# A scan that multiplies the sample state's decay on ScalarE, loads B, C and decay rows earlier, and squares later

## The chip, the cores and the metric

The kernel runs on one core of one Trainium2 chip. The metric is the device time of one launch in microseconds (us); the time before is the median of three runs. TensorE (PE in the profile, PEld its weight loads) multiplies matrices, VectorE (DVE), ScalarE (ACT) and GpSimd (POOL) do the elementwise work, SyncE (SP) issues the DMAs. Each has a queue of its own that runs in order. SBUF and PSUM are the two on-chip memories, PSUM the one that TensorE writes.

## The reference, cut to what matters

One layer of a decoder, for a prompt of 1024 tokens and a sample group of 8 sequences with one new token each, which share the weights. A projection of the normed input gives q, k, v for a dilated window attention and z, x, B, C, dt for a state-space scan (32 heads of 64, 8 groups of B and C, state size 128). The scan of the prompt runs in 8 chunks of 128 tokens; for the sample it is one step from a given state. Then come the gates, an output projection and an MLP, all in f32.

```python
# prompt, per chunk, group and head; a_cs is the running sum of dt * A
lmat = exp(segsum(a))                                   # decay from row s to row l
y_diag = einsum('bcgels,bcsgep->bclgep', cb * lmat, x * dt)
states = einsum('bclgn,bclgep->bcgepn', B, x * dt * exp(a_cs[last] - a_cs))
y_off  = einsum('bclgn,bcgepn->bclgep', C, state_before) * exp(a_cs)
# sample, one token: state (heads, 64, 128) of each of 8 sequences
state = state * exp(dt * A) + (x * dt) outer B          # written out as ssm_sample
y = state . C + d_skip * x
# both: y = rmsnorm_per_group(y * silu(z)) * norm_g
```

## The kernel before

All dense products run as `Dense` jobs: one job makes 128 output features for all tokens, in three chunks of 384, 384 and 264 tokens. A chunk is 24 matmuls into one PSUM tile (`mm`, three of them): each f32 operand is split into a high and a low part and three of the four products are added (lines 140 to 142). Weights are loaded (`wraw`), cast on ScalarE (`whi`, L94) and subtracted on GpSimd (`wlo`, L95), one job ahead. A chunk ends with its eviction (`evac`).

One chunk is one step of a clock. Everything that is not dense is written as generators (`sides`); after each chunk `pump` advances them, up to 4 turns a step in the scan, in the order of the list. `rest(n)` lets n steps pass. So the code sets where the small matmuls of the sides stand between the chunks. Only TensorE's order is taken as written (`manual_schedule`). The order on the other engines and on SyncE's DMA queue is made by the framework, which may run an instruction before others that stand ahead of it in the code, as far as data and buffers allow; a tile with `bufs=n` waits until its n-th predecessor is no longer needed.

The scan stage (474 to some 1275 us of the span) runs over 8 groups of 4 heads. In a group the dense work is 2 z jobs, then 4 x jobs of the next group (x, x, B, C; for five groups one gate job among them): 21 steps, some 108 us. The x eviction is a 4-tap causal convolution: ScalarE makes the first tap (L819), VectorE adds three (L823), ScalarE the tanh (L832), VectorE the product (L833). Results stand in `ck` tiles. Next to it run three generators for each group (`ssd_sides`):

- `chunks` goes through the 8 prompt chunks. `load(c)` fetches the decay row `ar` (4 heads x 128 tokens, the same row to all 128 partitions, 256 KB) from `ac_d` (L906, five buffers). `prep(c)` transposes x and B and multiplies C by B on TensorE, scales x on VectorE (L925, L928), and makes the decay matrix in place: four relus and an exp on ScalarE (L932, L934), a product on GpSimd (L935). `state(c)` makes the carried state (L941, L947), `out(c)` the outputs (L956, L960, then L964 to L967).
- `decode` updates the sample state, in four pairs of sequences `bh` and two halves t. B and C go through DRAM (`bc_d`) and come back to all partitions (`bc`, L867, two buffers); the state comes in `hst` (L872, four buffers) and goes out again (L892). VectorE makes dx = x dt (L884), ScalarE tmp = B dx (L887), VectorE hst = hst decay + tmp (L888) and the product with C (L890).
- `finish_` gates each of the three token chunks (`gate`: GpSimd's product L978, its store, ScalarE's squares L980, VectorE's sum L981) and two steps later adds the squares up on TensorE (`sums`).

Before the scan, the attention stage makes scores, softmax and values of 8 blocks for each of 6 head pairs (`attn_side`): L545 adds the bias, takes the maximum and writes it into the tile `o`, which also gets the values and is then stored to `att_d`; there are four such tiles. After the scan, the output projection's last jobs feed the second norm (`norm2`): the squares of 8 feature blocks are added in `ssq` (L1371), summed over features on TensorE (`rstd_cols`, L284), turned into a factor on VectorE, spread by transposes (L1420), and applied to 8 blocks (L1423 to L1429), which the MLP's first jobs read.

Of the kernel before, what the change touches and what calls it, by code (L numbers as in the profile page):

```python
# [7 lines left out]
F32 = mybir.dt.float32  # L8
# [3 lines left out]
OP = mybir.AluOpType  # L12
# [28 lines left out]
def _trunk(ctx, tc, nc, I, O):  # L41
# [109 lines left out]
    def rest(n):  # L151
        t = clock[0] + n
        while clock[0] < t:
            yield 'wait'
# [334 lines left out]
    def attn_side(u, tiles):  # L489
# [42 lines left out]
        def scores(j):  # L532
            nk = 128 * len(kbs[j])
            b0 = 128 if (g < 2 and nk == 128) else 0
            st = sts[j] = at.tile([128, 2, 256], F32, name="st", tag="st", bufs=4)
            o = os_[j] = at.tile([128, 132], F32, name="o", tag="o", bufs=4)
            lm = o[:, 128:132]
            nm = at.tile([128, 2], F32, name="nm", tag="nm", bufs=2)
            ps = [ps_(), ps_()]
            for hb in range(2):  # L540
                T.matmul(ps[hb][:, :nk], qt[hb * 64:(hb + 1) * 64, j * 128:(j + 1) * 128],  # L541
                         kt[hb * 64:(hb + 1) * 64, kbs[j][0] * 128:kbs[j][0] * 128 + nk],
                         start=True, stop=True)
            for hb in range(2):
                V.tensor_tensor_reduce(st[:, hb, :nk], ps[hb][:, :nk], bias[:, hb, b0:b0 + nk], 1.0, -3e38,  # L545
                                       OP.add, OP.max, lm[:, 2 + hb:3 + hb])
            V.tensor_scalar(nm, lm[:, 2:4], -1.0, None, op0=OP.mult)
            for hb in range(2):
                A.activation(st[:, hb, :nk], st[:, hb, :nk], AF.Exp, bias=nm[:, hb:hb + 1],
                             accum_out=lm[:, hb:hb + 1])  # L550
# [240 lines left out]
    def x_jobs(gi, tl):  # L791
# [45 lines left out]
            jobs.append(Dense(w_in, 0, col, 128, hx_, evac, halo=HALO))  # L837
        return jobs

    def ssd_sides(gi, tl):  # L840
        X, Z = tl['x'], tl['z']
        hs = slice(4 * gi, 4 * gi + 4)
# [6 lines left out]
        def decode():  # L849
            while tl['nx'] < 12:  # L850
                yield 'wait'
            yield from rest(1)
            tl['fin']()
            yield from rest(1)
            rb = sa.tile([11, 256], F32, name="rb", tag="tail", bufs=2)[:8].rearrange("p (k n) -> p k n", k=2)
            ps = ps_()
            T.transpose(ps[:8, 0:128], X[2][2][:, sam], ident)
            T.transpose(ps[:8, 128:256], X[3][2][:, sam], ident)
            V.tensor_copy(rb.rearrange("p k n -> p (k n)"), ps[:8, :256])
            dma(bc_d[gi].rearrange("k b n -> b k n"), rb)  # L860
            got = {}

            def load(bh):
                if bh > 3:
                    return
                bc = sd.tile([128, 2, 2, 128], F32, name="bc", tag="bc", bufs=2)
                dma(bc, dap(bc_d, gi * 2048 + bh * 256, [[0, 128], [1024, 2], [128, 2], [1, 128]]))  # L867
                hs_ = []
                for t in range(2):
                    r0 = bh * 2 * 262144 + (4 * gi + 2 * t) * 8192  # L870
                    hst = sd.tile([128, 2, 128], F32, name="hst", tag="hst", bufs=4)
                    dma(hst, dap(ws, r0, [[128, 128], [262144, 2], [1, 128]]))  # L872
                    hs_.append((r0, hst))
                got[bh] = bc, hs_
            load(0)
            yield from rest(2)
            for bh in range(4):
                load(bh + 1)
                bc, hs_ = got[bh]
                for t, (r0, hst) in enumerate(hs_):  # L880
                    ds = dsel[:, 2 * gi + t, :]
                    dx = sd.tile([128, 8], F32, name="dx", tag="dx", bufs=2)
                    xcol = X[t][2][:, 256 + 2 * bh:258 + 2 * bh]
                    V.tensor_tensor(dx[:, :2], xcol, ds[:, 2 * bh:2 * bh + 2], op=OP.mult)  # L884
                    for i in range(2):
                        tmp = sd.tile([128, 128], F32, name="tmp", tag="tmp", bufs=3)
                        A.mul(tmp, bc[:, 0, i, :], dx[:, i:i + 1])  # L887
                        V.scalar_tensor_tensor(hst[:, i, :], hst[:, i, :], ds[:, 8 + 2 * bh + i:9 + 2 * bh + i],  # L888
                                               tmp, op0=OP.mult, op1=OP.add)
                        V.tensor_tensor_reduce(tmp, hst[:, i, :], bc[:, 1, i, :], 1.0, 0.0,  # L890
                                               OP.mult, OP.add, dx[:, 4 + i:5 + i])
                    dma(dap(wso, r0, [[128, 128], [262144, 2], [1, 128]]), hst)  # L892
                    V.scalar_tensor_tensor(xcol, xcol, ds[:, 16:17], dx[:, 4:6], op0=OP.mult, op1=OP.add)
                yield from rest(2)
            tl['dec'] = 1

        A_, S_ = {}, {}

        D_ = {}

        def load(c):

            if c > 7:
                return
            ar = D_[c] = sd.tile([128, 4, 128], F32, name="ar", tag="ar", bufs=5)
            dma(ar, dap(ac_d, 4 * gi * 1024 + c * 128, [[0, 128], [1024, 4], [1, 128]]))  # L906

        def prep(c):
            ar = D_.pop(c)
            er = None  # L910
            if c:
                er = sd.tile([128, 2, 128], F32, name="er", tag="er", bufs=4)
# [61 lines left out]
        def gate(ci):  # L974
            t0, nt = CH[ci]
            sq = sq_[ci] = [sd.tile([128, 384], F32, name="sq", tag="sq", bufs=2) for _ in range(2)]
            for t in range(2):
                P.tensor_tensor(X[t][ci][:, :nt], X[t][ci][:, :nt], Z[t][ci][:, :nt], op=OP.mult)  # L978
                dma(y_d[2 * gi + t, :, t0:t0 + nt], X[t][ci][:, :nt])
                A.activation(sq[t][:, :nt], X[t][ci][:, :nt], AF.Square)  # L980
            V.tensor_tensor(sq[0][:, :nt], sq[0][:, :nt], sq[1][:, :nt], op=OP.add)  # L981
            if nt < 384:
                V.memset(sq[0][:, nt:], 0.0)
            live[ci // 2] -= 4
# [4 lines left out]
        def chunks():  # L989
            while gi and tls[gi - 1]['c'] < 8:  # L990
                yield 'wait'
            for c in range(4):
                load(c)
            while tl['nx'] < 12:
                yield 'wait'
            yield from rest(1)
# [6 lines left out]
            for c in range(8):  # L1003
                state(c)
                yield from rest(1)
                out(c)
                if c + 3 < 8:
                    prep(c + 3)
                load(c + 4)
                tl['c'] = c + 1  # L1010
                if c in (2, 5, 7):
                    live[c // 6] -= 2
                yield from rest(int(c % 3 < 2))
                yield
# [9 lines left out]
        def finish_():  # L1024
            for ci in range(3):
                while tl['c'] < min(8, 3 * ci + 3) or tl['nz'] < 6 or (ci == 2 and not tl['dec']):
                    yield 'wait'
                yield from rest(1)
                gate(ci)
                yield from rest(2)  # L1030
                sums(ci)
                yield
# [374 lines left out]
    def norm2(ci):  # L1407
# [4 lines left out]
            yield 'wait'  # L1412
        if nt < 384:
            V.memset(ssq[ci][:, nt:], 0.0)
        yield from rest(1)
        r = rstd_cols(ssq[ci], 1.0 / D, EPS, n2)
        yield from rest(1)
        ps = ps_()
# [238 lines left out]
```

## Time and profile before

| | us |
|---|---|
| median of 3 runs | 2441.43 (2438.29 to 2441.92) |
| the profiled execution | 2438.0 |
| its span, first to last instruction | 2435.3 |
| TensorE busy | 2331.7 (96%) |
| VectorE, ScalarE, GpSimd busy | 1191.1, 858.6, 692.8 |
| granted TensorE clock, mean | 0.980 |

In the rows below, times are us from the start of the span unless marked ns. A timeline row gives start, duration, engine, line, operation, tiles written <- read, shapes, count, and in brackets how long the engine had been idle before it and what ended that. Rows of waits give the total, the number of times and the longest. Rows of groups of instructions give count, busy us, mean ns, and the idle time before them with its releasers. A wait is put down to the signal that came last by the profile; where that had long been there, it was another.

### The profile page before, as it was taken

Reading aid. Unit: us, or ns where it says so; the run is one execution under the profiler, and the core shown is the slowest. Engines: PE = TensorE matmul, PEld = TensorE weight load, DVE = VectorE, ACT = ScalarE, POOL = GpSimd, SP = SyncE. Lnnn points to the kernel's source line nnn. Section 1 sums busy time; section 2 is a strip of 40 time slices with the busy share of each in tenths; the row PEclk is TensorE's granted clock in tenths of the full one; section 3 lists DMA queues with packets and bytes.
Section 4 is the critical chain, followed back from the end, with each engine's and each line's share of the span. In section 5 each row is a group of like instructions: output and inputs, shape, how many; then the busy total and the mean of one; then the engine's idle time right before and its main releaser. Section 6 shows DMA issues by size and latency. Waiting matters only on the chain.

```text
span 2435.3 us, 40623 instructions
## 1 busy us (share of the span) xinstructions
PE 2331.7 (96%) x15156; PEld 2228.4 (92%) x15156; DVE 1191.1 (49%) x3227; ACT 858.6 (35%) x2104; POOL 692.8 (28%) x645
## 2 busy tenths in 40 slices
PE   6989999999999999999999899999999999999997
PEld 4858888989889998989999899999999999999997
DVE  4533334576666657477655644546433333333336
ACT  5333433544445444354433331134221221221232
POOL 1202122233333333333343323441312212222230
PEclk8989999999999999999999999999999999999999
DMA  8355434354443434444445433340544444411111
GB/s 305 122 160 154 139 89 101 88 145 116 105 111 98 123 81 126 96 118 123 100 133 161 145 103 92 116 152 22 169 143 154 155 152 151 133 48 44 57 40 70
DMA packets 359571, 288.59 MB, mean 119 GB/s; under 512 B 24014, under 2 KB 350221, under 8 KB 353598
## 3 DMA queue, kind: packets, MB, share of 16 engines
q1 hardware_dynamic: 359374, 286.01, 40.2%
q8 instruction: 119, 1.95, 0.3%
q14 instruction: 78, 0.64, 0.1%
HBM read 243.77 MB, written 88.74 MB: 137 GB/s over the span
## 4 chain that ended last, share of the span: by engine, by line
PE 67%; DMA 12%; DVE 8%; ACT 4%; POOL 3%; issue 3%; SPq 2%; ACTq 0%; DVEq 0%; POOLq 0%
PE mm L140 20%; PE mm L141 20%; PE mm L142 20%; DMA ar<-ac_d 8%; DVE ck L823 2%; ACT ar L932 2%; PE ps L567 1%; POOL wlo L95 1%; DMA wada<-w_ada 1%; DMA bc<-bc_d 1%; PE ps L541 1%; DVE hst L888 1%; POOL ar L935 1%; DVE tmp L890 1%; PE ps L558 1%
## 5 line engine op out<-in xcount | busy, mean ns | idle before, releaser
L140 PE MATMUL mm<-hh,whi 128*128 128x384 f32 (+3 forms) x2784 | 922.2, 331 | 24.6 <-DVE ck L823 21.3
L141 PE MATMUL mm<-hl,whi 128*128 128x384 f32 (+3 forms) x2784 | 897.5, 322 | 0.8 <-DVE hl L413 0.7
L142 PE MATMUL mm<-hh,wlo 128*128 128x384 f32 (+3 forms) x2784 | 897.2, 322 | 0.0
L95 POOL TENSOR_TENSOR wlo<-wraw,whi 128x512 fp32r<-128x512 f32 x330 | 424.0, 1290 | 1175.9 <-ACT whi L94 1117.8
L140 PEld LDWEIGHTS mm<-hh,whi 128*128 128x128 f32 x2784 | 532.2, 191 | 37.5 <-issue 23.3
L141 PEld LDWEIGHTS mm<-hl,whi 128*128 128x128 f32 x2784 | 531.5, 191 | 3.3 <-DVE hl L413 1.2
L142 PEld LDWEIGHTS mm<-hh,wlo 128*128 128x128 f32 x2784 | 530.4, 191 | 0.0
L94 ACT CAST whi<-wraw 128x512 fp32r<-128x512 f32 x330 | 200.7, 611 | 462.2 <-PE mm L141 393.5
L1355 DVE SCALAR_TENSOR_TENSOR acc<-mm,mod,acc 128x384 f32<-128x384 f32 (+1 forms) x216 | 123.4, 572 | 230.5 <-PE mm L142 230.5
L141 PE MATMUL mm<-dl,whi 128*128 128x384 f32 (+1 forms) x696 | 223.4, 321 | 0.0
L142 PE MATMUL mm<-dh,wlo 128*128 128x384 f32 (+1 forms) x696 | 222.5, 320 | 0.0
L140 PE MATMUL mm<-dh,whi 128*128 128x384 f32 (+1 forms) x696 | 222.4, 320 | 0.0
L823 DVE SCALAR_TENSOR_TENSOR ck<-mm,cwT,ck 128x384 f32<-128x384 f32 (+4 forms) x288 | 163.0, 567 | 51.4 <-ACT ck L819 47.4
L1449 DVE TENSOR_TENSOR r<-r 128x384 f32<-128x384 f32 (+1 forms) x96 | 69.5, 724 | 185.7 <-ACT r L1448 185.7
L935 POOL TENSOR_TENSOR ar<-ar,cb 128x512 f32<-128x512 f32 x64 | 84.3, 1322 | 181.1 <-DVE cb L930 171.6
L140 PEld LDWEIGHTS mm<-dh,whi 128*128 128x128 f32 x696 | 131.1, 188 | 0.0
L141 PEld LDWEIGHTS mm<-dl,whi 128*128 128x128 f32 x696 | 131.0, 188 | 0.0
L142 PEld LDWEIGHTS mm<-dh,wlo 128*128 128x128 f32 x696 | 130.9, 188 | 0.0
L932 ACT ACTIVATE ar<-ar,acs 128x128 f32<-128x128 f32 x256 | 85.9, 392 | 125.9 <-DMA ar<-ac_d 117.1
L888 DVE SCALAR_TENSOR_TENSOR hst<-hst,dsel,tmp 128x128 f32<-128x128 f32 x128 | 66.4, 539 | 67.0 <-ACT tmp L887 61.6
L1448 ACT ACTIVATE r<-mm 128x384 f32<-128x384 f32 (+1 forms) x96 | 43.8, 456 | 153.4 <-PE mm L142 152.8
L832 ACT ACTIVATE th<-ck 128x384 f32<-128x384 f32 (+1 forms) x96 | 47.2, 492 | 107.4 <-DVE ck L823 107.4
(366 smaller groups left out, 3383.0 us busy)
## 6 DMA issues: line engine op xcount, KB each, us to landing
wraw<-w_in SPq DMA_DIRECT2D x164, 256.0 KB
kv_g_sample<-cache_kv_g SPq DMA_DIRECT2D x144, 256.0 KB
wada<-w_ada SPq DMA_DIRECT2D x24, 1024.0 KB
ar<-ac_d SPq DMA_DIRECT2D x64, 256.0 KB
wraw<-w_up SPq DMA_DIRECT2D x64, 256.0 KB
wraw<-w_down SPq DMA_DIRECT2D x58, 256.0 KB
hst<-state_ssm SPq DMA_DIRECT2D x64, 128.0 KB
bc<-bc_d SPq DMA_DIRECT2D x32, 256.0 KB
```

The costliest lines, as they stand in the source:

```text
L94: A.copy(hi, raw)
L95: P.tensor_tensor(lo, raw, hi, op=OP.subtract)
L140: T.matmul(ps[:n, :m], wh, a, start=(k == 0), stop=False)
L141: T.matmul(ps[:n, :m], wh, b, start=False, stop=False)
L142: T.matmul(ps[:n, :m], wl, a, start=False, stop=(k == nk - 1))
L823: V.scalar_tensor_tensor(acc[:, o:n], ps[:, x0 + o - d:x0 + n - d], w[k], acc[:, o:n], op0=OP.mult, op1=OP.add)
L832: A.activation(th[:, :nt], acc[:, :nt], AF.Tanh)
L888: V.scalar_tensor_tensor(hst[:, i, :], hst[:, i, :], ds[:, 8 + 2 * bh + i:9 + 2 * bh + i], tmp, op0=OP.mult, op1=OP.add)
L932: A.activation(ar[:, h, :], ar[:, h, :], AF.Relu, bias=acs[:, c, 4 * gi + h:4 * gi + h + 1], scale=-1.0)
L935: P.tensor_tensor(ar, ar, cb[:, None, :].to_broadcast([128, 4, 128]), op=OP.mult)
L1355: V.scalar_tensor_tensor(x[:, t0:t0 + n], ps[:, :n], gate[:, 0:1], x[:, t0:t0 + n], op0=OP.mult, op1=OP.add)
L1449: V.tensor_tensor(r[:, :nt], r[:, :nt], r[:, :nt], op=OP.mult)
```

## The change

`decode` multiplies the state tile by its decay on ScalarE, in place; VectorE then adds B times dx to it. B, C and state are loaded two pairs ahead (three and six buffers), the first work comes five steps after the first load instead of two, and each half pair has a step of its own. The decay rows get eight buffers, and `out(c)` is followed by the load of the same chunk of the next group; the first group's eight are loaded at the start. In `gate` a step passes between GpSimd's products and the squares. `o` of the attention gets eight tiles. `norm2` lets two steps pass before its sums.

```diff
--- before.py
+++ after.py
@@ -533,7 +533,7 @@
             nk = 128 * len(kbs[j])
             b0 = 128 if (g < 2 and nk == 128) else 0
             st = sts[j] = at.tile([128, 2, 256], F32, name="st", tag="st", bufs=4)
-            o = os_[j] = at.tile([128, 132], F32, name="o", tag="o", bufs=4)
+            o = os_[j] = at.tile([128, 132], F32, name="o", tag="o", bufs=8)
             lm = o[:, 128:132]
             nm = at.tile([128, 2], F32, name="nm", tag="nm", bufs=2)
             ps = [ps_(), ps_()]
@@ -837,6 +837,8 @@
             jobs.append(Dense(w_in, 0, col, 128, hx_, evac, halo=HALO))
         return jobs
 
+    D_ = {}
+
     def ssd_sides(gi, tl):
         X, Z = tl['x'], tl['z']
         hs = slice(4 * gi, 4 * gi + 4)
@@ -863,19 +865,20 @@
             def load(bh):
                 if bh > 3:
                     return
-                bc = sd.tile([128, 2, 2, 128], F32, name="bc", tag="bc", bufs=2)
+                bc = sd.tile([128, 2, 2, 128], F32, name="bc", tag="bc", bufs=3)
                 dma(bc, dap(bc_d, gi * 2048 + bh * 256, [[0, 128], [1024, 2], [128, 2], [1, 128]]))
                 hs_ = []
                 for t in range(2):
                     r0 = bh * 2 * 262144 + (4 * gi + 2 * t) * 8192
-                    hst = sd.tile([128, 2, 128], F32, name="hst", tag="hst", bufs=4)
+                    hst = sd.tile([128, 2, 128], F32, name="hst", tag="hst", bufs=6)
                     dma(hst, dap(ws, r0, [[128, 128], [262144, 2], [1, 128]]))
                     hs_.append((r0, hst))
                 got[bh] = bc, hs_
             load(0)
-            yield from rest(2)
+            load(1)
+            yield from rest(5)
             for bh in range(4):
-                load(bh + 1)
+                load(bh + 2)
                 bc, hs_ = got[bh]
                 for t, (r0, hst) in enumerate(hs_):
                     ds = dsel[:, 2 * gi + t, :]
@@ -884,29 +887,26 @@
                     V.tensor_tensor(dx[:, :2], xcol, ds[:, 2 * bh:2 * bh + 2], op=OP.mult)
                     for i in range(2):
                         tmp = sd.tile([128, 128], F32, name="tmp", tag="tmp", bufs=3)
-                        A.mul(tmp, bc[:, 0, i, :], dx[:, i:i + 1])
-                        V.scalar_tensor_tensor(hst[:, i, :], hst[:, i, :], ds[:, 8 + 2 * bh + i:9 + 2 * bh + i],
-                                               tmp, op0=OP.mult, op1=OP.add)
+                        A.mul(hst[:, i, :], hst[:, i, :], ds[:, 8 + 2 * bh + i:9 + 2 * bh + i])
+                        V.scalar_tensor_tensor(hst[:, i, :], bc[:, 0, i, :], dx[:, i:i + 1], hst[:, i, :],
+                                               op0=OP.mult, op1=OP.add)
                         V.tensor_tensor_reduce(tmp, hst[:, i, :], bc[:, 1, i, :], 1.0, 0.0,
                                                OP.mult, OP.add, dx[:, 4 + i:5 + i])
                     dma(dap(wso, r0, [[128, 128], [262144, 2], [1, 128]]), hst)
                     V.scalar_tensor_tensor(xcol, xcol, ds[:, 16:17], dx[:, 4:6], op0=OP.mult, op1=OP.add)
-                yield from rest(2)
+                    yield from rest(1)
             tl['dec'] = 1
 
         A_, S_ = {}, {}
 
-        D_ = {}
-
-        def load(c):
-
-            if c > 7:
-                return
-            ar = D_[c] = sd.tile([128, 4, 128], F32, name="ar", tag="ar", bufs=5)
-            dma(ar, dap(ac_d, 4 * gi * 1024 + c * 128, [[0, 128], [1024, 4], [1, 128]]))
+        def load(g, c):
+
+            if g < 8:
+                ar = D_[g, c] = sd.tile([128, 4, 128], F32, name="ar", tag="ar", bufs=8)
+                dma(ar, dap(ac_d, 4 * g * 1024 + c * 128, [[0, 128], [1024, 4], [1, 128]]))
 
         def prep(c):
-            ar = D_.pop(c)
+            ar = D_.pop((gi, c))
             er = None
             if c:
                 er = sd.tile([128, 2, 128], F32, name="er", tag="er", bufs=4)
@@ -977,6 +977,8 @@
             for t in range(2):
                 P.tensor_tensor(X[t][ci][:, :nt], X[t][ci][:, :nt], Z[t][ci][:, :nt], op=OP.mult)
                 dma(y_d[2 * gi + t, :, t0:t0 + nt], X[t][ci][:, :nt])
+            yield from rest(1)
+            for t in range(2):
                 A.activation(sq[t][:, :nt], X[t][ci][:, :nt], AF.Square)
             V.tensor_tensor(sq[0][:, :nt], sq[0][:, :nt], sq[1][:, :nt], op=OP.add)
             if nt < 384:
@@ -989,8 +991,9 @@
         def chunks():
             while gi and tls[gi - 1]['c'] < 8:
                 yield 'wait'
-            for c in range(4):
-                load(c)
+            if gi == 0:
+                for c in range(8):
+                    load(0, c)
             while tl['nx'] < 12:
                 yield 'wait'
             yield from rest(1)
@@ -1006,7 +1009,7 @@
                 out(c)
                 if c + 3 < 8:
                     prep(c + 3)
-                load(c + 4)
+                load(gi + 1, c)
                 tl['c'] = c + 1
                 if c in (2, 5, 7):
                     live[c // 6] -= 2
@@ -1026,7 +1029,7 @@
                 while tl['c'] < min(8, 3 * ci + 3) or tl['nz'] < 6 or (ci == 2 and not tl['dec']):
                     yield 'wait'
                 yield from rest(1)
-                gate(ci)
+                yield from gate(ci)
                 yield from rest(2)
                 sums(ci)
                 yield
@@ -1412,7 +1415,7 @@
             yield 'wait'
         if nt < 384:
             V.memset(ssq[ci][:, nt:], 0.0)
-        yield from rest(1)
+        yield from rest(2)
         r = rstd_cols(ssq[ci], 1.0 / D, EPS, n2)
         yield from rest(1)
         ps = ps_()
```

## Rows read from the trace of the kernel before

**Rows 1.** Busy time by stretch: stretch, length, each engine's busy us (instructions), clock, DMA.

```profile
474.00:1240.00 766.00, 730.84 (x4855) 700.25 (x4854) 496.37 (x1436) 359.38 (x935) 282.35 (x254) 0.98 0.44 113
...
724.00:734.00 10.00, 7.52 (x34) 6.94 (x34) 8.29 (x22) 5.04 (x12) 2.31 (x3) 0.66 0.29 81
```

**Rows 2.** What TensorE waited for, 474 to 1240 us.

```profile
PE mm L140 <- DVE ck L823: 21.3, 12, 2.4
PE ps L956 <- DVE state L947: 7.6, 4, 2.6
...
PE ps L284 <- DVE sq L981: 1.7, 1, 1.7
```

**Rows 3.** Groups of instructions in the scan, ScalarE and VectorE.

```profile
L932 ACT ACTIVATE ar<-ar,acs 128x128 f32<-128x128 f32 x256 | 85.9, 392 | 125.9 <-DMA ar<-ac_d 117.1 <-PE ps L960 4.6 <-POOL state L944 2.6
L888 DVE SCALAR_TENSOR_TENSOR hst<-hst,dsel,tmp 128x128 f32<-128x128 f32 x128 | 66.4, 539 | 67.0 <-ACT tmp L887 61.6 <-DMA hst<-state_ssm 3.8
L887 ACT ACTIVATE tmp<-bc,dx 128x128 f32<-128x128 f32 x128 | 45.6, 393 | 58.1 <-DMA bc<-bc_d 38.2 <-DVE dx L884 15.6 <-DVE dx L890 3.0
...
L980 ACT ACTIVATE sq<-ck 128x384 f32<-128x384 f32 (+1 forms) x48 | 22.5, 487 | 33.4 <-POOL ck L978 33.3
```

**Rows 4.** Timelines of ScalarE and TensorE, 850 to 855 us.

```profile
850.27 0.40 ACT L932 ACTIVATE ar<-ar,acs 128x128 f32<-128x128 f32 x1 [3.33 <-DMA ar<-ac_d]
...
851.61 0.65 ACT L819 ACTIVATE ck<-mm,vecT,cwT 128x384 f32<-128x384 f32 x1
...
854.36 0.41 PE L140 MATMUL mm<-hh,whi 128*128 128x384 f32 x1 [2.07 <-DVE ck L823]
```

**Rows 5.** Timelines of ScalarE, VectorE and TensorE, 831 to 835 us.

```profile
831.40 1.28 ACT L932 ACTIVATE ar<-ar,acs 128x128 f32<-128x128 f32 x4 [3.03 <-DMA ar<-ac_d]
832.59 0.39 ACT L887 ACTIVATE tmp<-bc,dx 128x128 f32<-128x128 f32 x1
...
833.01 0.35 DVE L888 SCALAR_TENSOR_TENSOR hst<-hst,dsel,tmp 128x128 f32<-128x128 f32 x1 [1.78 <-DMA hst<-state_ssm]
...
834.65 0.68 PE L956 MATMUL ps<-ck,state 128*128 128x128 f32 x4 [1.46 <-DVE state L947]
```

**Rows 6.** Timelines of TensorE, SyncE and ScalarE: one decay row's buffer, load, relu and use.

```profile
876.01 0.66 PE L960 MATMUL ps<-ar,xd 128*64 128x128 f32 x8
880.86 0.46 SPq L906 DMA_DIRECT2D ar<-ac_d  x1
886.52 0.40 ACT L932 ACTIVATE ar<-ar,acs 128x128 f32<-128x128 f32 x1 [2.44 <-DMA ar<-ac_d]
...
954.84 0.66 PE L960 MATMUL ps<-ar,xd 128*64 128x128 f32 x8
```

**Rows 7.** What SyncE's queue waited for, 474 to 1240 us.

```profile
SPq L872 <- DMA ssm_sample<-hst: 39.9, 28, 4.2
```

**Rows 8.** Timeline of ScalarE, 886 to 889 us.

```profile
886.83 0.72 ACT L980 ACTIVATE sq<-ck 128x264 f32<-128x264 f32 x2
...
888.04 0.65 ACT L819 ACTIVATE ck<-mm,vecT,cwT 128x384 f32<-128x384 f32 x1
```

**Rows 9.** Timeline of TensorE in the attention stage, its two waits for `o`.

```profile
161.81 0.33 PE L517 MATMUL ps<-cst,big 128*128 128x128 f32 x1 [2.87 <-DVE o L545]
...
182.97 0.33 PE L517 MATMUL ps<-cst,big 128*128 128x128 f32 x1 [1.29 <-DVE o L545]
```

**Rows 10.** Second norm: TensorE's waits; timelines of VectorE and TensorE, 1698 to 1710 us.

```profile
PE ps L284 <- DVE ssq L1371: 4.1, 2, 2.3
...
1698.10 0.43 DVE L1423 TENSOR_TENSOR ht<-acc,ps 128x264 f32<-128x264 f32 x1 [3.34 <-PE ps L1420]
...
1706.28 0.28 PE L140 MATMUL mm<-hh,whi 128*128 128x264 f32 x1
...
1709.04 0.42 DVE L1429 TENSOR_TENSOR hl<-ht,hh 128x264 fp32r<-128x264 f32 x1
```

## The prediction

> **What bounds the kernel now.** I read the page first, then the waits of TensorE, then the stretches by stage, and last the timelines round the gaps. TensorE is busy nearly everywhere; only its gaps, and the clock that falls after them, can be won. In the scan (474 to 1240 us, where nearly all of the change lies) it is idle for 766 - 730.8 = 35.2 us, and the granted clock averages 0.98, so that (1 - 0.98) x 766 = 15 us more pass at the lower of the two levels, 1.2 GHz for 2.4 GHz [rows 1]. The whole pool there is some 50 us, 2% of the time. Two gaps head the list: 21.3 us in 12 pieces in which a dense matmul waits for a PSUM tile that VectorE empties late (L823), and 7.6 us in 4 pieces in which the scan's matmul waits for the carried state (L947) [rows 2]. Neither VectorE nor ScalarE is full in this stage (496 and 359 of 766 us [rows 1]); they are late because their queues run in order and something at the head waits. ScalarE's worst: 117.1 us before the relu over a decay row `ar` (L932) whose load has not landed [rows 3].
>
> The reader can see both forms. At 850.27 ScalarE has sat 3.33 us before such a relu; the eviction behind it (L819) starts at 851.61, VectorE's taps follow, and TensorE's next chunk starts 2.07 us late at 854.36 [rows 4]. The same 2.07 us returns in other groups. At 831.40 it has sat 3.03 us; behind it the multiply L887 for the sample state starts at 832.59, VectorE's L888 waits for that (1.78 us; the row names a DMA, but the tile it reads is the one L887 writes), and the carried state behind L888 leaves TensorE idle for 1.46 us [rows 5].
>
> **The change part by part.** The profiled execution took 2438.0 us (2435.3 of span); the median of the three runs is 2441.4. I add up gains as seen in the profile and take them off the median.
>
> *Decay rows a group ahead (5 to 8 buffers).* This aims at the 117.1 us, and I cost it at nothing. Only TensorE's order is written out; on the other engines, and on the DMA queue, instructions run ahead of the code as soon as a buffer allows. Take the 37th load (chunk 4 of group 4): it may go once chunk 7 of group 3 has been multiplied at 876.01 and freed a buffer; it is issued at 880.86, by the code some two chunks into group 4; its relu stands right behind the landing, at 886.52, and even so ScalarE has waited 2.44 us; the matmul that needs it comes at 954.84 [rows 6]. There were 68 us to spare and ScalarE waited all the same, because the relu follows the load in its queue. With eight buffers each `out(c)` frees one and one load goes, as now; the relu stands behind it, as now. What changes is the label. Each load on the SyncE queue waits for a matmul that has just been written down, but that is the wait it has today. At the start three more loads of 256 KB go at once; nothing on TensorE waits then, so 0.
>
> The Trainium skill ("Perfetto Trace Analysis", Optimization Strategy) says that consistent bubbles, the same gap repeating on the engine that should be full, can mean too few buffers. By that rule the 2.07 us would go with the deeper ring, and the sum below would win some 30 us more: the first rival gives it from the rows. For attention's `o`, below, the trace agrees with the rule (gaps of 2.87 and 1.29 us); for `ar` the 68 us speak against it.
>
> *Decay on ScalarE, sum on VectorE.* Counts stay: 128 ScalarE multiplies of 393 ns, 128 VectorE sums of 539 ns, which still read two tensors [rows 3]. What falls is the round trip: today VectorE makes dx, ScalarE multiplies B by it, VectorE waits (61.6 us before L888), and ScalarE waits 38.2 us for B and C and 15.6 us for dx [rows 3]. Afterwards ScalarE needs the state tile alone, early, and VectorE needs B, C and dx. The wait for the first B, C of a group (the 38.2 us) passes from ScalarE to VectorE, which is idle there anyway. B, C two steps ahead and six state tiles keep the rest fed, so I expect the state update to end sooner than today, in spite of its later place in the code (first pair five steps after B, C are asked for, not two; then a step for each half pair; by the code it still ends two steps before the last chunk). With that, L888 no longer stands behind a blocked relu: the 7.6 us [rows 2] go, with the 0.34 x 10 = 3.4 us of low clock after the longest of them [rows 1], 11 at most, 0 at least; I take 8.
>
> New is that ScalarE can wait for the state's load: those multiplies, too, will stand right behind the landing, a group ahead. No row shows that wait. SyncE holds state loads back for 39.9 us in 28 waits until the older tile has been stored [rows 7], so they do come late. Lower bound 0. Upper: as with the relus. Their 117.1 us cost TensorE at most 21.3 + 7.6 us of gaps and 15 us of clock, 44 us, or 0.38 us for each us of ScalarE's waiting; 64 state loads against 64 decay rows would cost 44 once more. A state load is half as large (128 against 256 KB) and reads each byte once, so I take a small part, 3 us lost.
>
> *Squares a step behind the gate.* ScalarE sits 33.3 us before squares whose product GpSimd has not finished [rows 3]. By the code the squares now come behind the next eviction: at 886.83 two of them (0.72 us) ran ahead of the eviction at 888.04 [rows 8], which the late chunk at 890 then waited for. Some 0.7 us in four or five groups: 3 us, from 0 to all of the 21.3. The sums on TensorE move a step later as well: the one gap there (1.7 us, first group [rows 2]) goes, with up to 3.4 us of low clock if it costs what the row from 724 shows; 3, from 0 to 5.
>
> *Attention's `o` from 4 to 8 tiles.* Twice TensorE waits for scores held up by the store of an old `o`: 2.87 and 1.29 us [rows 9]. With eight tiles the store is five steps old. 4.2 us, with up to 3.4 of clock; I take 5, from 0 to 7.6.
>
> *Second norm a step later.* TensorE waits 4.1 us twice over for the sums of squares [rows 10]. These waits go, but not the time: behind the last of them eight features pass through VectorE, ScalarE and GpSimd from 1698.10 to 1709.46, and the chunk that reads them already starts at 1706.28, before the last is there [rows 10]. That work starts when it does now, so the chunk will wait for it. I take 2, from -2 to 7.5.
>
> Sum: 8 - 3 + 3 + 3 + 5 + 2 = 18 us. 2441.4 - 18 = **2423 us**.
>
> **The rivals.** (1) *The prefetch does what it says.* For it: the gaps repeat at the same place. Against it: the 68 us to spare [rows 6]. Then the 21.3 us go with the clock that is not counted yet (15 - 3.4 - 3.4 = 8): 30 us less the 3 already taken, 2441 - 18 - 27 = 2396 (2385 to 2409).
>
> (2) *Nothing to see*: the waits that go are followed at once by the next one in the queue, as the relus stay and the squares and the state's multiplies only trade places with evictions. Then only attention is left, and the new wait takes that: about 2440.
>
> (3) *Slower: ScalarE stuck behind the state's loads.* The place: L887's successor, six tiles of which are multiplied a group ahead, each behind a load that waits for a store that waits for VectorE. They fall into the steps of [rows 5], as the x chunks begin to need ScalarE for their evictions. For it: SyncE's 28 waits [rows 7], and that the relus already show what such a place costs. Against it: the state update flows more freely, and the tiles are small. At 0.38 us each, the other gains (21 us) are used up when ScalarE waits 55 us in all, 0.9 us a load; at 1.6 us a load it is 39 us: 2441 + 18 = 2459 (2448 to 2475).
>
> **How the numbers follow.** Forecast 0.45 (2410 to 2435), the prefetch works 0.15, nothing 0.18, slower 0.22. A measurement of this kernel tells about 0.2% (5 us) from no change. Faster by more than that: 0.45 + 0.15 = 0.60; within: 0.18; slower: 0.22. The range 2396 to 2456 leaves out the lower half of the first rival and nearly half of the third, some 0.17.
>
> **What would show it.** Right: ScalarE's wait for `ar` stays near 100 us and the 2.07 us gaps with it; the gaps before the state matmul (L956) are gone; no wait of attention's scores for a store; the third norm's chunk waits for its own tiles. Wrong: the wait for `ar` falls under 40 us (first rival); ScalarE waits over 55 us for `hst`, and dense matmuls wait more than 21.3 us for L823 (third rival); the state update ends later than some 30 us after the group's B, C were written.

## The result and the profile after

| | before | after |
|---|---|---|
| median of 5 runs | 2441.92 (2438.29 to 2448.34) | 2460.66 (2455.32 to 2468.49) |
| ratio, 95% interval | | 1.0082 (1.0065 to 1.0100) |
| the profiled execution, its span | 2438.0, 2435.3 | 2468.49, 2466.7 |
| TensorE idle, 474 to 1240 us | 35.2 | 51.2 |
| granted clock there | 0.98 | 0.97 |

The change makes the kernel slower by 0.8%, some 20 us; 2423 was predicted, with a range of 2396 to 2456. The profiled execution of the changed kernel is the slowest of its five, so its trace shows 31 us more than that of before, not 20. (A yardstick for such differences: in the second norm's experiment below, whose scan is the code of before, the last output of the scan stood 5.9 us earlier than in the trace of before.) By the places of the same matmuls in the two traces, the attention stage ends 0.2 us earlier and the scan 21 us later; the merge (of the attention's parts, right behind the scan) adds some 3 us, and what follows up to the down projection another 7.

The changed kernel by stretch (as [rows 1]: the stretch, its length, busy us of TensorE, its loads, VectorE, ScalarE and GpSimd, the clock):

```profile
474.00:1240.00 766.00, 714.83 (x4693) 686.86 (x4692) 477.49 (x1367) 356.39 (x927) 274.87 (x247) 0.97 0.43 111
```

And its waits in the same stretch (engine, line, what it waited for, total us, times, longest); the first two answer to [rows 2], the next four to [rows 3], the last to [rows 7]:

```profile
PE mm L140 <- DVE ck L823: 46.2, 20, 4.3
PE ps L956 <- ACT hst L890: 1.1, 1, 1.1
...
ACT ar L932 <- DMA ar<-ac_d: 116.2, 37, 5.8
DVE ck L823 <- ACT ck L819: 100.8, 34, 11.2
DVE hst L891 <- DMA bc<-bc_d: 37.4, 8, 5.6
ACT hst L890 <- DMA hst<-state_ssm: 12.0, 14, 2.2
...
SPq L874 <- DMA ssm_sample<-hst: 44.5, 19, 5.0
```

The gaps before the state matmul (L956) went, 7.6 to 1.1 us. The gaps before dense matmuls that wait for the taps (L823) more than doubled, 21.3 to 46.2. The decay row's wait did not move, and ScalarE waits only 12 us for state tiles. (The 117.1 us of [rows 3], and its 33.3 us before the squares, run on to 1290; up to 1240, where the waits below are taken too, the kernel before has these:)

```profile
ACT ar L932 <- DMA ar<-ac_d: 114.5, 40, 6.1
ACT sq L980 <- POOL ck L978: 24.0, 22, 3.4
```

One place, on ScalarE, VectorE and TensorE of the changed kernel:

```profile
1061.19 0.70 ACT L890 ACTIVATE hst<-hst,dsel 128x128 f32<-128x128 f32 x2 [1.69 <-DMA hst<-state_ssm]
1065.05 1.28 ACT L932 ACTIVATE ar<-ar,acs 128x128 f32<-128x128 f32 x4 [3.16 <-DMA ar<-ac_d]
1066.37 0.63 ACT L934 ACTIVATE ar<-ar 128x512 f32<-128x512 f32 x1
1066.91 0.66 ACT L819 ACTIVATE ck<-mm,vecT,cwT 128x384 f32<-128x384 f32 x1
...
1067.60 1.92 DVE L823 SCALAR_TENSOR_TENSOR ck<-mm,cwT,ck 128x381 f32<-128x381 f32 x3 [4.35 <-ACT ck L819]
...
1069.66 0.66 PE L140 MATMUL mm<-hh,whi 128*128 128x384 f32 x1 [3.84 <-DVE ck L823]
```

It is the picture of [rows 4], longer. The x chunk ended on TensorE at 1058.93; its eviction (L819) starts 8 us later. Ahead of it ScalarE sits first before the state's multiply (1.69 us), then before the relu (3.16 us). Both belong to the next group (6, while group 5's chunks run) and both stand right behind a load. In the 12 us ahead of each of the 20 late evictions behind these gaps ScalarE sat before a relu, and ahead of six of them also before a multiply.

### The profile page after: what moved, and what is told of

It reads as the page before. It is cut to its first block, busy times and chain, and to the rows that moved or that the text cites. A ratio compares the mean times of both kernels' runs of the same rounds, so it can differ in the third digit from the quotient of the medians.

```text
span 2466.7 us, 40615 instructions
## 1 busy us (share of the span) xinstructions
PE 2342.6 (95%) x15156; PEld 2239.2 (91%) x15156; DVE 1191.8 (48%) x3227; ACT 861.0 (35%) x2104; POOL 692.7 (28%) x645
## 4 chain that ended last, share of the span: by engine, by line
PE 70%; DMA 11%; DVE 8%; ACT 4%; issue 3%; POOL 3%; SPq 1%; DVEq 0%; ACTq 0%; POOLq 0%
PE mm L140 21%; PE mm L141 21%; PE mm L142 21%; DMA ar<-ac_d 6%; DVE ck L823 2%; PE ps L567 1%; ACT ar L932 1%; DMA qb<-qkv_d 1%; DMA wada<-w_ada 1%; DMA bc<-bc_d 1%; PE ps L541 1%; DVE hst L891 1%; DMA ssm_sample<-hst 1%; POOL wlo L95 1%; DMA hst<-state_ssm 1%
## 5 line engine op out<-in xcount | busy, mean ns | idle before, releaser
L140 PE MATMUL mm<-hh,whi 128*128 128x384 f32 (+3 forms) x2784 | 928.5, 334 | 49.6 <-DVE ck L823 46.2
L823 DVE SCALAR_TENSOR_TENSOR ck<-mm,cwT,ck 128x384 f32<-128x384 f32 (+4 forms) x288 | 163.2, 568 | 108.8 <-ACT ck L819 104.2
L932 ACT ACTIVATE ar<-ar,acs 128x128 f32<-128x128 f32 x256 | 85.6, 395 | 125.3 <-DMA ar<-ac_d 116.2
L833 DVE SCALAR_TENSOR_TENSOR ck<-th,ck 128x384 f32<-128x384 f32 (+1 forms) x96 | 64.6, 674 | 38.8 <-ACT th L832 37.8
```

Of the source, the lines that this page charges most:

```text
L140: T.matmul(ps[:n, :m], wh, a, start=(k == 0), stop=False)
L823: V.scalar_tensor_tensor(acc[:, o:n], ps[:, x0 + o - d:x0 + n - d], w[k], acc[:, o:n], op0=OP.mult, op1=OP.add)
L833: V.scalar_tensor_tensor(acc[:, :nt], th[:, :nt], 1.0, acc[:, :nt], op0=OP.add, op1=OP.mult)
L932: A.activation(ar[:, h, :], ar[:, h, :], AF.Relu, bias=acs[:, c, 4 * gi + h:4 * gi + h + 1], scale=-1.0)
```

## The experiments

A hold below means that the instruction may not run ahead of a named one on its engine; lines shift by one to three where code was added. Times in us that stand beside a ratio are the ratio's share of 2438. The ranges in the expectations were set from a before of some 2441; the kernel before that ran beside each experiment took 2434 to 2440, so the ratio decides. The diffs give the edits in short form.

**The parts one by one.** First the swap alone in the kernel before (`ds_decay` stands for the decay's column of `ds`):

```diff
-A.mul(tmp, bc[:, 0, i, :], dx[:, i:i + 1])
-V.scalar_tensor_tensor(hst, hst, ds_decay, tmp, op0=OP.mult, op1=OP.add)
+A.mul(hst, hst, ds_decay)
+V.scalar_tensor_tensor(hst, bc[:, 0, i, :], dx[:, i:i + 1], hst, op0=OP.mult, op1=OP.add)
```

> The kernel before with the swap alone: ScalarE multiplies the state by its decay, VectorE adds B dx; loads, buffers and steps of the sample state as before. Theory A (the multiplies stand behind the state's loads in ScalarE's queue, and hold back the x evictions): ScalarE waits 10 to 25 us for hst, TensorE waits for L823 over 30 us (21.3 before), time 2450 to 2462. Rival B (the later, spread plan of the sample state costs it, the swap itself is sound): the gaps at L956 go, no more waits at L823, time 2430 to 2441.

Measured: 2452.77, ratio 1.0063 (1.0044 to 1.0081), 15 us slower. Waits, 474 to 1240 (L887 is now the state's multiply):

```profile
ACT ar L932 <- DMA ar<-ac_d: 127.2, 39, 5.9
PE mm L140 <- DVE ck L823: 38.4, 19, 4.3
ACT hst L887 <- DMA hst<-state_ssm: 3.0, 5, 1.3
```

Dense matmuls wait 38.4 us for L823, as theory A asked. But ScalarE waits only 3.0 us for state tiles, under what it asked for; its wait for decay rows rose from 114.5 to 127.2 us. In the 12 us ahead of each of the 19 late evictions behind these gaps ScalarE had sat before a relu; before a state's multiply it had sat ahead of one of them, for 1.3 us. So the gaps still hang on the relus.

The plan of the sample state alone:

```diff
-bufs=2 (bc), bufs=4 (hst), rest(2), load(bh + 1), rest(2) for each pair
+bufs=3 (bc), bufs=6 (hst), load(1), rest(5), load(bh + 2), rest(1) for each half pair
```

> The kernel before with the new plan of the sample state alone: B, C and state loaded two pairs ahead (3 and 6 buffers), first work five steps after the load, a step for each half pair; ScalarE still makes B dx. Theory A: within 5 us of before (2437 to 2447). Rival B (the plan costs it): 2450 to 2465, TensorE's waits for L823 over 30 us although no multiply stands behind a state load.

Measured: 2443.71, 1.0035 (1.0019 to 1.0051), 8 us slower by the ratio, 5 by the medians: at the edge of what theory A allows and less than rival B asks. The interval does not reach 1, so the plan costs too, but how much is not sharp. Its profiled execution was its longest (2454), so no row of it is used here.

Both together:

> Swap and plan together, no other part. Theory A: slower like the swap alone or more, since six state tiles are multiplied further ahead: 2452 to 2464, the sum of L823 waits 35 to 50 us, ScalarE's wait for hst 10 to 20 us. Rival B: as the plan alone, whatever that gives. Rival C (it is the eight decay rows or the squares that cost): within 5 us of before.

Measured: 2444.67, 1.0030 (1.0015 to 1.0044), 7 us: as the plan alone, which is rival B, and less than the swap alone. The two do not add: where the plan is, the swap costs nothing more that can be measured, and wins nothing.

The eight decay rows alone (the diff of L906 and of the calls of `load`):

> The kernel before with eight decay rows, loaded a group ahead, and nothing else. As predicted (the relu follows its load in the queue): ScalarE still waits 95 to 130 us for ar, TensorE's waits for L823 stay at 18 to 26 us, time 2436 to 2446. Rival C (three more rows in flight delay other loads, relus come a group early and stand ahead of more evictions): 2447 to 2462. First rival of the prediction (the prefetch works): wait for ar under 40 us, 2410 to 2420.

Measured: 2438.78, 1.0002 (0.9989 to 1.0015). Waits in its scan, 474 to 1240:

```profile
ACT ar L931 <- DMA ar<-ac_d: 115.6, 41, 5.5
PE mm L140 <- DVE ck L823: 21.9, 13, 2.5
```

These are the rows of before, 114.5 and 21.3. More buffers and a load a group ahead change nothing by themselves.

Squares a step later alone:

> The kernel before with the squares (and so the sums) a step later, nothing else. The prediction's term: 3 us for the squares out of the evictions' way and 3 for the sums: 2431 to 2440, ScalarE's wait for squares behind GpSimd under 10 us. Rival A: the framework runs the squares when their product is there, whatever the step, so the wait stays at 20 to 30 us and the time within 5 us of before. Rival B (what is missing of the change's loss, once the sample state's 7 us and the second norm are taken off, lies here: later squares collide with the next evictions): 2444 to 2452.

Measured: 2440.70, 1.0019 (1.0008 to 1.0030), 5 us slower. ScalarE's wait before the squares, 474 to 1240:

```profile
ACT sq L982 <- POOL ck L978: 24.0, 22, 3.4
```

It is the wait of before to the tenth: rival A's mechanism, with a loss at the edge of its 5 us, and less than rival B asked. At the end of the scan its trace stands within 1 us of that of before. The loss comes behind it: from the scan's last output to the merge's last matmul it takes 90.8 us, before 88.4. The six traces with later squares take 89.9 to 91.2 us there, the other thirteen 87.3 to 89.7. So about half of the 5 us lies there, and the change's 3 us in the merge with it; why it costs there is not shown.

The second norm's `rest(2)` alone:

> The kernel before with the second norm's sums a step later and nothing else. Theory from the changed kernel's trace (the waits for sums stay and the following chunk waits for its own tiles, with more low clock): 2443 to 2450, all of it lost between 1690 and 1740. The prediction's term (2 gained): 2436 to 2441. Rival (in the changed kernel it was the odd phase after the scan that cost, not the step): within 3 us of before.

Measured: 2440.01, 1.0021 (1.0010 to 1.0031), 5 us slower. TensorE's waits there, 1640 to 1740 us (before: 4.1 us in all, [rows 10]):

```profile
PE ps L284 <- DVE ssq L1371: 3.2, 2, 1.8
PE mm L141 <- DVE hl L1429: 1.2, 3, 0.5
PE mm L141 <- POOL hl L1429: 0.8, 1, 0.8
```

The waits for the sums shrink by 0.9 us, and the chunk that needs the normed tiles now waits for them, 2.2 us with 0.2 for L1428. That is a loss of 1.3 us in gaps; from the merge's last matmul to the down projection's first, this execution takes 2.5 us longer than that of before. From the norm's last transposes (L1420) to the down projection's first matmul the thirteen traces without this step take 37.2 us each, the six with it 39.0 to 40.5 (39.0 here, 40.4 in the changed kernel), so 2 to 3 us of the loss lie there. What is left of the 5 us it doesn't show.

All of the change but squares and norm:

> The change without the later squares and without the later second norm (swap, plan, rows and o stay). If the parts add up: 2444 to 2453, the rest of the 19 us being the squares' 5 and the norm's 5. If they do not (squares and multiplies hurt each other only when together, or not at all): 2436 to 2443, or 2454 to 2461.

Measured: 2450.85, 1.0056 (1.0036 to 1.0075), 14 us. With 5 each for squares and norm that gives some 23 against the 20 measured; from swap and plan together it is 7 + 0 + 5 + 5 = 17. Within the intervals the change is swap and plan, squares and norm. The 14 against the 7 of swap and plan alone stand at the edge of their intervals: whether eight rows and `o` cost something beside them stays open.

**Holding the relus.** Eight decay rows, and the four relus and the exp held behind the copy of B^T of the same chunk:

```diff
-A.copy(bt, pt[:, 256:384])
+bi = A.copy(bt, pt[:, 256:384])
...
+with tc.issue_after(bi.ins):
     (four relus over ar, L932; exp over ar, L934)
```

> The kernel before with the eight decay rows loaded a group ahead, and the four relus and the exp of a chunk held behind the copy of B^T of the same chunk (L927) on ScalarE, so that they can't run ahead of their place in the code. Theory (the relu waits because it follows its load in ScalarE's queue; each us of that costs TensorE some 0.38 us): ScalarE's wait for ar under 30 us (117 before), TensorE's waits for L823 under 12 us (21.3), time 2405 to 2428. Rival (the wait is only where ScalarE idles anyway, and the evictions are late for another reason): wait for ar gone, waits for L823 at 17 to 25, time within 6 us of before. Second rival (held relus make the outputs' decay matrix late): TensorE waits at L960 or the relus pile up before an eviction, 2445 or more.

Measured: 2381.28, ratio 0.9779 (0.9765 to 0.9794), 54 us faster, beyond the theory's best. Then the hold alone, with the five rows of before:

> The kernel before with the relus and the exp held behind the copy of B^T of their chunk, and nothing else: five decay rows, each loaded four chunks ahead as before. Theory P (both halves are needed: the held relu leaves the row to land in time only if the load starts early): some of ScalarE's wait for ar comes back (20 to 60 us), time 2395 to 2425. Theory Q (the place of the relu is all, the deeper ring does nothing even now): as the held kernel with eight rows, 2376 to 2390, wait for ar under 15 us.

Measured: 2380.75, 0.9764 (0.9743 to 0.9786), theory Q. Its scan by stretch, its only wait of ScalarE for a row, and one row's load (SyncE) and relu (ScalarE):

```profile
474.00:1240.00 766.00, 766.00 (x5244) 741.36 (x5243) 525.06 (x1501) 375.11 (x973) 307.00 (x276) 1.00 0.46 123
```

```profile
ACT ar L933 <- DMA ar<-ac_d: 1.8, 1, 1.8
```

```profile
883.38 0.42 SPq L906 DMA_DIRECT2D ar<-ac_d  x1
...
907.70 0.61 ACT L94 CAST whi<-wraw 128x512 fp32r<-128x512 f32 x1
908.21 0.25 ACT L927 COPY bt<-ps 128x128 f32<-128x128 f32 x1
908.36 1.28 ACT L933 ACTIVATE ar<-ar,acs 128x128 f32<-128x128 f32 x4
909.55 0.55 ACT L819 ACTIVATE ck<-mm,vecT,cwT 128x256 f32<-128x256 f32 x1
```

TensorE is busy for all 766 us at a granted clock of 1.00: the whole pool of [rows 1] is won. (To the scan's last output this trace is 56.6 us shorter than that of before: 35.2 us of gaps and some 21 us of busy time, where the prediction put 15 us down to the clock.) The row was asked for 25 us before its relu, where [rows 6] had 5.7; the load had always been early enough, the relu was too early.

The changed kernel with the relus held:

> The changed kernel with the relus and the exp held in the same way. Theory: the 116 us wait for ar goes under 30, TensorE's waits for L823 fall from 46 to 20 to 32 us (what the state's multiplies cost stays), time 2430 to 2448. Rival (the relus' wait is harmless): within 6 us of the changed kernel's 2461. Second rival (the relus alone carry the loss, the state's multiplies only lengthen their wait): 2410 to 2428, as the held kernel without the swap.

Measured: 2397.81, 0.9847 (0.9833 to 0.9860): 37 us under before and, by the two ratios, 57 under the changed kernel as it was, faster than any of the three expected, but 17 us above the hold without the other parts. Its waits, 474 to 1240:

```profile
ACT hst L890 <- DMA hst<-state_ssm: 57.8, 25, 5.6
PE mm L140 <- DVE ck L823: 5.3, 5, 1.7
```

With the relus out of the way, the state's multiplies take their place at the head of ScalarE's queue: 12.0 us of waiting become 57.8.

**Holding the multiplies.** The swap alone again, now with its multiplies held behind ScalarE's part of the last dense eviction:

```diff
-A.mul(hst, hst, ds_decay)
+with tc.issue_after(last_eviction.ins):
+    A.mul(hst, hst, ds_decay)
```

> The kernel before with the swap, its decay multiplies held behind ScalarE's part of the last dense eviction; relus free as before. Theory A (the swap alone cost 15 us because the multiplies run ahead of the evictions into ScalarE's queue): 2432 to 2443, waits for L823 back at 18 to 27 us (38 with the swap alone). Theory D (the swap cost because ScalarE no longer waits for B, C and so reaches the blocked relus sooner; the multiplies' place does not matter): stays at 2447 to 2458, ScalarE's wait for ar stays at 125 to 145 us.

Measured: 2425.87, 0.9946 (0.9928 to 0.9964), 13 us faster than before. With free multiplies it was 15 us slower, so their place is worth 28 us, more than theory A asked. Its waits:

```profile
ACT ar L935 <- DMA ar<-ac_d: 158.5, 48, 6.8
PE mm L140 <- DVE ck L825: 15.6, 9, 2.2
```

ScalarE waits 44 us longer for rows than before, and TensorE less for L823: the sum of an engine's waits is no measure of what they cost. That it counts on which side of an x eviction a wait falls is my reading, and not shown. All of TensorE's gaps in the scan fell by 1.7 us only (35.2 to 33.5; a single wait of 5.9 us for dx is new); some 10 us of the gain are busy time.

The swap with relus held and multiplies free:

> The kernel before with the relus held and the swap, multiplies free. Theory A (free multiplies cost by themselves, behind state loads): 2387 to 2398, ScalarE's wait for hst over 30 us. Rival (they hurt only where relus are blocked as well): 2376 to 2384.

Measured: 2409.31, 0.9899 (0.9874 to 0.9924), slower than theory A's range. And with both held:

> The kernel before with relus held and with the swap, its multiplies held too. If the swap is sound by itself (VectorE no longer waits for ScalarE's product): 2368 to 2379, under the 2381 of the held relus alone. If there is nothing left to win in the scan (TensorE waits there already under 2 us for L823): 2379 to 2386.

Measured: 2379.04, 0.9761 (0.9746 to 0.9776). Free against held multiplies is some 33 us here. In the free one ScalarE waits 52.6 us for state tiles, and TensorE for the sums behind late squares:

```profile
ACT hst L887 <- DMA hst<-state_ssm: 52.6, 23, 5.7
PE ps L284 <- DVE sq L982: 10.1, 7, 1.7
PE mm L140 <- DVE ck L823: 4.1, 5, 1.3
```

The clock is 0.98 there and 1.00 where the relus alone were held. With both held the time is that of the held relus alone: the swap then wins nothing that can be measured.

The changed kernel with both held:

> The changed kernel with relus and exp held as before and the state's multiplies held too, behind ScalarE's part of the last dense eviction. With the relus held alone it took 2398 us, ScalarE waiting 57.8 us for state tiles. Theory A (that wait is what still parts it from the 2381 us of the held kernel without the rest): wait for hst under 25 us, 2380 to 2392. Rival (what parts them are the squares, the second norm and the later plan): 2393 to 2402.

Measured: 2387.53, 0.9794 (0.9774 to 0.9814), theory A; dense matmuls wait 0.6 us for L823. By the ratios another 13 us come from the multiplies; some 7 above the 2381 stay with the other parts.

Last, the changed kernel with the multiplies held and the relus free:

> The changed kernel with the state's multiplies held behind ScalarE's part of the last dense eviction, relus free. Theory A (their place is what costs): the 20 to 27 us that the same hold won with the swap alone come back here: 2434 to 2445, waits for L823 from 46 to under 30 us. Rival (with six tiles, later steps and squares the loss is spread, the multiplies are only one part): 2446 to 2456.

Measured: 2457.23, 1.0090 (1.0068 to 1.0112): nothing won, against theory A and a little above the rival. One of its long gaps (ScalarE, VectorE, TensorE):

```profile
879.68 1.28 ACT L935 ACTIVATE ar<-ar,acs 128x128 f32<-128x128 f32 x4 [5.47 <-DMA ar<-ac_d]
881.00 0.63 ACT L937 ACTIVATE ar<-ar 128x512 f32<-128x512 f32 x1
881.53 0.66 ACT L821 ACTIVATE ck<-mm,vecT,cwT 128x384 f32<-128x384 f32 x1
...
882.22 0.61 DVE L825 SCALAR_TENSOR_TENSOR ck<-mm,cwT,ck 128x381 f32<-128x381 f32 x1 [9.73 <-ACT ck L821]
...
884.69 0.56 PE L140 MATMUL mm<-hh,whi 128*128 128x384 f32 x1 [3.59 <-DVE ck L825]
```

Here the relu alone blocks ScalarE ahead of the eviction (143.9 us of waiting for rows in all, 116.2 with free multiplies). That row's buffer was free at 862.41, its load issued at 873.35, behind stores and state loads in SyncE's queue. So I tried eight state tiles in the changed kernel:

```diff
-hst = sd.tile([128, 2, 128], F32, name="hst", tag="hst", bufs=6)
+hst = sd.tile([128, 2, 128], F32, name="hst", tag="hst", bufs=8)
```

> The changed kernel with eight state tiles for six, so that a state load never waits for a store of its own group. Theory S (SyncE's in-order queue, stopped by state loads that wait for stores, makes the decay rows late and so the relus): SyncE's wait at the state load from 45 under 15 us, ScalarE's wait for ar under 100 us, time 2440 to 2453. Rival (the rows are late for other heads of that queue as well, stores and gate products, and a state load that comes earlier is multiplied earlier): wait for ar 105 to 140, time 2454 to 2466.

Measured: 2455.44, 1.0084 (1.0066 to 1.0101), the rival; SyncE's wait at the state loads stays (41.6 us from 474 to 1275, 44.9 with six tiles), and now all of a group's multiplies run a whole group ahead, where twelve of sixteen did with six tiles (SyncE, ScalarE, VectorE; the tile's load, multiply and sum):

```profile
597.87 0.97 SPq L874 DMA_DIRECT2D hst<-state_ssm  x2
...
605.34 0.39 ACT L890 ACTIVATE hst<-hst,dsel 128x128 f32<-128x128 f32 x1
...
706.24 0.62 DVE L891 SCALAR_TENSOR_TENSOR hst<-bc,dx,hst 128x128 f32<-128x128 f32 x2 [5.28 <-DMA bc<-bc_d]
```

The multiply runs 101 us before its result is wanted, in a step where evictions want ScalarE. The wait that theory S names was not taken away, so this neither shows nor refutes it.

**Attention's `o`,** eight tiles beside eight rows and held relus:

> Eight decay rows, relus held, and eight tiles o in the attention; nothing else of the change. Prediction's term for o: 5 us less than the same without it (2381), so 2374 to 2379, and no wait of scores (L517) for a store. Rival (the changed kernel's trace: the gap goes, another takes its place before the stage ends): 2379 to 2384.

Measured: 2380.99, 0.9762 (0.9743 to 0.9781), against 0.9779 and 0.9764 without it. The two waits of [rows 9] shrink to one of 0.6 us, but a gain from 0 to some 4 us can't be told apart here.

## Why the prediction was wrong

*Right.* That the deeper ring leaves the relus' wait as it is, for the reason given: 114.5 before, 116.2 and, alone, 115.6 us. The Trainium skill ("Perfetto Trace Analysis", Optimization Strategy) says that consistent bubbles can mean too few buffers; for the decay rows the measurement says otherwise, since eight rows gave 1.0002 and a hold with five rows took all of the gaps away. That the gaps at L956 go. That the state update is sooner done: the last store of a group comes 26 to 30 us after B, C are written, before 29 to 33 (first group left out). That the chunk behind the second norm waits for its own tiles.

*The step that failed* is first the sample state: swap and plan were to win 8 - 3 = 5 us and lose 7 (1.0030), 12 of the 38 us between forecast and measurement. Both of its halves were wrong. The plan I counted as help, at no cost of its own; alone it costs some 8 us (1.0035). And the swap's 5 us did not come: on top of the plan it gives nothing (1.0030 against 1.0035). I took the gaps before the state matmul (L956) for won time; they went, and others took their place before L823.

The price of the multiplies' new place, 3 us, fails too. I had bounded it at 44 us and took 3 because the tiles are small. Without the plan it measures 28 us with the relus free (1.0063 against 0.9946) and some 33 with them held. With the relus held the mechanism is the one I named, 52.6 us of waiting behind the state's loads. With them free it is not: the swap alone cost 15 us with 3.0 us of waiting for state tiles, and its late evictions stand behind relus. So my conversion, 0.38 us of TensorE for each us of ScalarE's waiting, was no fit measure; with held multiplies the waits for rows even grew by 44 us while the time fell. That held the swap gave 13 us, near my 8, is in good part luck: the gaps I had meant to win explain under 2 us of it, and with the relus held it gave nothing.

*The other terms.* Squares and sums, +3 and +3, measured -5: 11 us of the miss. I had the squares fall behind the next eviction because the code says so, although I had just argued for the relus that ScalarE does not keep to the code's order; the squares' wait did not move (24.0 us). The second norm, +2, measured -5, under its bound of -2: 7 us; its gaps (1.3 us) explain only part of that. `o`, +5, measured 0 to 4. Together with the sample state this is 31 to 35 of the 38 us; the rest is not assigned. The 5 us of squares and norm are no larger than what I had called the limit of a measurement; the intervals do not reach 1, and the traces show about half of each.

*The third rival* gave 2459 and the time came out at 2461, but that is luck. Of its two signs one came, L823 over 21.3 us; for the other it asked for over 55 us of waiting for state tiles, and 12 were there. Its mechanism, ScalarE stuck behind the state's loads, is shown with held relus. In the kernel before, only that the multiplies' place costs is shown, and in the whole change not even that: there the swap adds nothing to the plan (1.0035 and 1.0030), and holding the multiplies alone won nothing (1.0090 against 1.0082), while holding the relus won 57 us and both 70. What holds the gaps there are the relus, which were there before; the multiplies count only once these are out of the way.

*Open.* Why the plan costs 8 us by itself, though ScalarE's product there still needs B, C and so can't run ahead of them; why free multiplies cost so much without it, by way of the relus; whether SyncE's queue makes the rows of the changed kernel later, since the run meant to tell it did not take the queue's wait away; and what the later squares do behind the scan.

*The pool.* I put it at some 50 us and the held relus won 54 to 58: all of it, and some 6 us more in busy time than I had counted. My first rival gave 27 us beyond the forecast for a prefetch that works; it had the right place and the wrong lever.

## What to carry to other kernels

Where a scheduler lets instructions run ahead, one that needs nothing but a load can stand right behind that load at the head of its engine's queue. Here more buffers left its wait as it was (114.5 and 115.6 us); an order took it away (1.8 us). Look for a wait on a DMA by an instruction whose result is wanted tens of us later: give the instruction an order, not the load more room. Before you move work to an engine, ask what each moved instruction still waits for; if it is only a load, price it by the evictions it can stand before, not by its own waiting.

## What was not expected of the hardware

The clock followed the gaps closely: with the scan's gaps gone, the granted clock there read 1.00 for all 766 us, where 35.2 us of gaps had left it at 0.98 and 51.2 us at 0.97. Nothing was done for the clock itself; up to the scan's last output TensorE's busy time fell by some 21 us, where the prediction put 15 down to the clock. That all 21 are the clock's is not shown.
